# A two-layer hybrid block in fp32: the rests of block-product chunks behind the next down weights, and a block-product chunk in the first net

## The chip, the cores and the metric

The kernel runs on one core of one Trainium2 chip. A time is the device time of one execution in microseconds (us), and less is better. Several executions are given by their median. A profiled execution has a time of its own and a trace; the span is the stretch that the trace covers.

## The reference

All is fp32. One sequence of 256 tokens with 1024 features runs through two layers. This is the reference, cut to what matters here:

```python
def swiglu(x, w_gate, w_up, w_down):
    return (jax.nn.silu(x @ w_gate) * (x @ w_up)) @ w_down

for l in range(DEPTH):                       # DEPTH = 2, D_MODEL = 1024, D_FF = 2816
    h = layer_norm(ALPHA * h + 0.5 * swiglu(h, ffn1_gate[l], ffn1_up[l], ffn1_down[l]), ln_g[l, 0], ln_b[l, 0])
    z = h @ w_in[l]
    ...                                      # convolution, recurrence and pooling over parts of z
    h = layer_norm(ALPHA * h + mix, ln_g[l, 1], ln_b[l, 1])
    h = layer_norm(ALPHA * h + cross_attn(h, mem, ca_q[l], ca_k[l], ca_v[l], ca_o[l]), ln_g[l, 2], ln_b[l, 2])
    h = layer_norm(ALPHA * h + 0.5 * swiglu(h, ffn2_gate[l], ffn2_up[l], ffn2_down[l]), ln_g[l, 3], ln_b[l, 3])
```

`mem` has 256 rows of 1024. The change lies in `swiglu`, of which there are four; they are called nets here, and the first net is `ffn1` of layer 0.

## The kernel before

**Products.** An fp32 product is made of three TensorE (PE) products of parts. `split` makes the parts: ScalarE (ACT) casts the operand to a high part (L61), and VectorE (DVE) subtracts that from the operand for the low part (L62). Then high by high, high by low and low by high are added up in PSUM (`mm_rows`, all through L105). x is kept in such parts (`xTh`, `xTl`, both named xT in the profile). Weights come by DMA from SP's queue into a ring of six tiles `raw` (128x1024, 512 KB each), and their parts go into rings of eight `whi` and eight `wlo`. A DMA into `raw` must wait until both halves of the split have read the tile. PSUM has four `acc` and four `dn` tiles.

**A net.** D_FF is cut into five chunks of 512 columns and a last one of 256. A chunk c is made of x's products with gate and with up, then silu, then the product of the two; the outcome is turned so that its features lie across partitions: `turn` deals it out by four DMAs on SP (L450), DVE transposes it (L453), and it is split to `ah` and `al`. The down product then takes it in two halves, `both(c, 0)` and `both(c, 1)`. Each half is a slab of two weight tiles and 24 PE products, and all of them add to the four `dn` tiles. The program writes the half `both(c-2, 1)` and then `both(c-1, 0)` behind chunk c, so the down weights run about one chunk behind.

A chunk is made in one of two ways. `hidden` is the plain one: 48 PE products for gate and 48 for up. DVE multiplies at L440. `by_seven` takes gate and up together as a matrix of two by two blocks (`w00`, `w01`, `w10`, `w11`: gate and up, upper and lower half of x's features), x as two by two quarters, and makes their product by seven block products of 12 PE products each, 84 in all. For that DVE adds weight blocks to each other in place (L578), splits the sums as well (14 splits, where the plain chunk has 8), and combines the seven results (`put`, L600) into `e`, `f` and the two `g`; silu (L626) and a multiplication (L627) follow, then `turn`. `blocks_of_x` makes the four combinations of x's quarters that this needs (L536, L544 and a split each) and keeps them in `kTh` and `kTl`, which are otherwise used for the attention. Two of the quarters in fp32 are left over from the LayerNorm that made x (`pend(q[0:2])`).

```python
            sevens = (2, 4) if early is None else ()
```

So the third and fifth chunks of nets two to four are made by seven, and no chunk of the first net. `by_seven` loads its eight weight tiles into `spare0`, `spare1`, `spare2`, `lng`, `lnb` (tiles that LayerNorm's rows and other things use at other times) and three of `raw`.

**Beside it in the first net.** `early` is a function that only the first net gets. It issues the small parameters' and the memory's DMAs on GpSimd (POOL) behind the second chunk's weights (L193 for the memory, 32 of them), with the memory going to `spare0` and `spare1` (named m) and the parameters to `spare2`, and returns the `rest`: DVE's small steps and the memory's turning (L202, and four splits to mT). The rest is written behind the third chunk. `ln_params` loads the net's LayerNorm rows into `lng` and `lnb`, in the first net at c = 1, in the others at c = 5.

**Order.** A scheduler sets each engine's order from the program's order, with the dependences and buffers; every engine then runs its own list in order and waits at each entry for what it needs. `tc.issue_after` holds a piece back behind a given instruction, and in a `tc.manual_schedule` the written order stands.

Of the kernel before, what the change touches and what calls it, by code (L numbers as in the profile page):

```python
# [8 lines left out]
F32 = mybir.dt.float32  # L9
F32R = mybir.dt.float32r  # L10
U8 = mybir.dt.uint8
AF = mybir.ActivationFunctionType
# [5 lines left out]
P = 128  # L18
# [28 lines left out]
def model(ctx: ExitStack, tc: tile.TileContext, t: dict, out: bass.AP):  # L47
# [352 lines left out]
    def ffn(l, name, n, pend=None, last=False, early=None):  # L400
        gate, up, down = (t[f"{name}_{x}"][l] for x in ("gate", "up", "down"))
        with tc.tile_pool(name="ffn", bufs=2, reuse_waits="tile") as fp:
# [24 lines left out]
            def ordered(v):  # L427
                return v.rearrange("p (a k j) -> p k a j", a=4, j=32)
# [30 lines left out]
            def first():  # L459

                s = activations()
                wg = load(gate, 0, NK, 0, CHUNK, fine=pend is None)
                wu = load(up, 0, NK, 0, CHUNK) if pend is not None else None

                if pend is None:
                    idle = kTh[:, 0:2, :].rearrange("p k c -> p (k c)")
                    nc.vector.memset(idle.bitcast(F32), 0.0)

                    def busy(n):

                        for _ in range(n):
                            nc.tensor.matmul(blank, idle[:, 0:P], idle, start=True, stop=True)

                    with tc.manual_schedule(engines={E.Activation, E.DVE, E.PE}):
                        blank = acc((P, 512), "dn")
                        og = [acc((P, CHUNK), "dn") for _ in range(NT)]

                        def group(k, *tiles):
                            for i in tiles:
                                products(og[i], wg, i, k)  # L480

                        busy(5)
# [12 lines left out]
                        group(1, 1)  # L495
                        for k in range(2, NK):
                            if k + 1 < NK:
                                split(*wg.todo[k + 1])
                            group(k, 0, 1)
                    wu = load(up, 0, NK, 0, CHUNK)  # L500
                    ou = all_products(wu)
                    for i in range(NT):
                        activate(s, i, og[i])
                        gated(s, i, ou[i])
                else:
                    for i in range(NT):
                        og = acc((P, CHUNK))
                        for k in range(NK):
                            products(og, wg, i, k)
                        activate(s, i, og)  # L510
                        ou = acc((P, CHUNK))
                        for k in range(NK):
                            if i == 0 and k == NK // 2:
                                pend(q[0:2] if sevens else None)
# [4 lines left out]
            def hidden(c0):  # L519
# [11 lines left out]

            def blocks_of_x():

                for n, i, j in ((2, 0, 0), (3, 0, 1)):
                    part = (slice(None), slice(4 * j, 4 * j + 4), tok(i))
                    nc.vector.tensor_tensor(q[n], xTh[part].bitcast(F32), xTl[part].bitcast(F32), op=ALU.add)  # L536
                parts = [
                    tuple(y[:, 2 * n : 2 * n + 2, :].rearrange("p k (h t) -> p (k h) t", t=P) for y in (kTh, kTl))
                    for n in range(4)
                ]  # L540
                for n, o, a, b, op in (
                    (0, 1, 0, 1, ALU.subtract), (2, 0, 2, 0, ALU.subtract), (1, 2, 1, 2, ALU.subtract), (3, 3, 3, 2, ALU.add)
                ):
                    nc.vector.tensor_tensor(q[o], q[a], q[b], op=op)  # L544
                    split(*parts[n], q[o])
                return parts

            def by_seven(c0, bx):
# [50 lines left out]
                def put(o, a, op, b):  # L599
                    nc.vector.tensor_tensor(halves(o), sums(a), halves(b), op=op)  # L600
# [22 lines left out]
                s = fp.tile([P, NT, CHUNK], F32, tag="spare2", name="sg", bufs=1)  # L623
                for i, u in enumerate((e, f)):
                    v = ordered(s[:, i, :])
                    nc.scalar.activation(v, g[i].rearrange("p (k a j) -> p k a j", a=4, j=32), AF.Silu)  # L626
                    nc.vector.tensor_tensor(v, v, u.rearrange("p (k a j) -> p k a j", a=4, j=32), op=ALU.mult)  # L627
                return turn(s)

            def last_hidden(c0):  # L630

# [24 lines left out]
            if sevens:  # L656

                d = [fp.tile([P, DM], F32, tag=f"spare{n}", name="quarters", bufs=1) for n in range(2)]
                q = [d[n // 2].rearrange("p (n k t) -> p n k t", n=2, t=P)[:, n % 2] for n in range(4)]

            chunks = [(c, min(CHUNK, DFF - c)) for c in range(0, DFF, CHUNK)]

# [6 lines left out]
            def both(c, u):  # L669
                a = slab(c, u)  # L670
                for i in range(NT):
                    for k in range(2):
                        for m in range(2):
                            apart = last and i == m == k == u == 1 and c == 3
                            rows_of(a, i, k, m, c == u == k == 0, apart)

            for c, (c0, ncol) in enumerate(chunks):
                if not c:
                    acts.append(first())
                    ys = [[acc((P, 512), "dn") for _ in range(2)] for _ in range(NT)]  # L680
# [4 lines left out]
                if sevens and c == 1 and early is None:  # L685
                    bx = blocks_of_x()
                if c == (max(sevens) + 1 if sevens else 1):
                    gb = ln_params(l, n)
                if c == 1 and early is not None:

                    with tc.issue_after(loads[-1].ins):
                        rest = early(fp)
                if c == 2 and early is not None:
                    with tc.issue_after(lows[-1].ins):
                        for f in rest:
                            f()
                    if sevens:
                        bx = blocks_of_x()
# [485 lines left out]
```

## Time and profile before

| what | us |
|---|---|
| median of 3 runs | 1079.32 |
| lowest, highest | 1079.08, 1080.74 |
| profiled execution | 1079.12 |
| its span | 1077.2 |

In the profiled execution the granted TensorE clock was 0.999 of full speed, the program had 16293 instructions, and the DMA engines moved 231.9 MB, a mean of 215 GB/s. Rows of the profile name the line of the code, the engine, the operation, the tile written and, behind the arrow, the tiles read. A row of single instructions has its start in us and its duration first, and in brackets the idle time just before it and what ended that. PEld are PE's weight loads. Where a row stands for several instructions, x and their number follow.

### The profile page before, as it was taken

The page shows a single profiled execution, that of the slowest core. Times are in us where ns is not written, and L with a number is a line of the kernel's source. Part 1 is how long each engine was busy: PE and PEld are TensorE (multiplying, and loading weights), DVE is VectorE, ACT ScalarE, POOL GpSimd, SP SyncE. Part 2 cuts the span into 40 slices and gives each one's busy share as a digit, 9 for nine tenths or more (in the row PEclk, how much of TensorE's full clock was granted, in tenths as well). Part 3 has the DMA queues.
Part 4 walks back from the last instruction along what each step waited for, and adds up shares of the span by engine and source line. Part 5 has one row for each costly group of instructions (what it writes and reads, how often), then busy time and mean ns, then how long its engine had stood idle before and what let it go on. Part 6 is the DMA issues. An engine that isn't in the chain of part 4 may idle for free.

```text
span 1077.2 us, 16293 instructions
## 1 busy us (share of the span) xinstructions
PE 1064.0 (99%) x5979; PEld 939.5 (87%) x5979; DVE 921.3 (86%) x1287; ACT 630.2 (59%) x907; POOL 63.3 (6%) x114
## 2 busy tenths in 40 slices
PE   9999999999999999999999999999999999999997
PEld 7888888989899888888888888888898998888886
DVE  5758566998998799999799989888989787998986
ACT  6546454757467565555575556566764665655561
POOL 9600001000000000000000000010000000000000
PEclk9999999999999999999999999999999999999999
DMA  9997774754575575847675774956546665759371
GB/s 363 289 283 221 218 215 141 250 195 157 177 270 172 180 250 197 272 174 213 248 259 191 246 261 151 303 177 231 174 141 212 242 229 177 254 158 333 115 234 40
DMA packets 130895, 231.90 MB, mean 215 GB/s; under 512 B 9408, under 2 KB 48608, under 8 KB 130816
## 3 DMA queue, kind: packets, MB, share of 16 engines
q1 hardware_dynamic: 129024, 228.49, 64.9%
q0 software_dynamic: 1216, 1.20, 0.4%
q10 hardware_dynamic: 576, 1.18, 0.3%
q8 instruction: 47, 0.77, 0.3%
q14 instruction: 32, 0.26, 0.1%
HBM read 216.15 MB, written 1.05 MB: 202 GB/s over the span
## 4 chain that ended last, share of the span: by engine, by line
PE 88%; DVE 9%; issue 2%; ACT 0%; DMA 0%; DVEq 0%; ACTq 0%
PE acc L105 56%; PE dn L105 29%; DVE wlo L62 4%; DVE raw L578 2%; PE acc L172 1%; DVE half L600 1%; DVE square L453 1%; PE dn L886 1%; DVE al L62 1%; DVE sg L600 1%; DMA h<-in_x_dram 0%; PE dn L945 0%; ACT whi L61 0%; DVE sg L440 0%; DVE sg L627 0%
## 5 line engine op out<-in xcount | busy, mean ns | idle before, releaser
L61 ACT CAST whi<-raw 128x1024 fp32r<-128x1024 f32 (+1 forms) x432 | 435.3, 1042 | 227.6 <-DVE raw L578 74.0
L62 DVE TENSOR_TENSOR wlo<-raw,whi 128x1024 fp32r<-128x1024 f32 (+1 forms) x432 | 510.1, 1211 | 68.0 <-ACT whi L61 63.0
L105 PE MATMUL acc<-whi,xT 128*128 128x512 f32 x1072 | 324.6, 380 | 0.0
L105 PEld LDWEIGHTS acc<-whi,xT 128*128 128x128 f32 x1072 | 202.6, 189 | 28.6
L105 PE MATMUL acc<-wlo,xT 128*128 128x512 f32 x536 | 203.1, 379 | 0.0
L105 PE MATMUL acc<-xT,whi 128*128 128x512 f32 x576 | 142.2, 382 | 0.2
L105 PE MATMUL dn<-wlo,ah 128*128 128x512 f32 x346 | 131.8, 381 | 3.2 <-DVE wlo L62 3.2
L105 PE MATMUL dn<-whi,al 128*128 128x512 f32 x346 | 131.1, 379 | 0.0
L105 PE MATMUL dn<-whi,ah 128*128 128x512 f32 x346 | 130.5, 380 | 0.0
L105 PEld LDWEIGHTS acc<-xT,whi 128*128 128x128 f32 x576 | 103.9, 190 | 12.6 <-ACT whi L61 0.8
L105 PEld LDWEIGHTS acc<-wlo,xT 128*128 128x128 f32 x536 | 101.3, 189 | 14.5
L105 PE MATMUL dn<-whi,xT 128*128 128x512 f32 x288 | 88.4, 381 | 0.0
L105 PEld LDWEIGHTS acc<-xT,wlo 128*128 128x128 f32 x576 | 75.5, 191 | 3.9
L105 PEld LDWEIGHTS dn<-wlo,ah 128*128 128x128 f32 x346 | 65.4, 189 | 14.7 <-DVE wlo L62 5.6
L105 PE MATMUL acc<-xT,wlo 128*128 128x256 f32 x576 | 75.9, 275 | 0.0
L105 PEld LDWEIGHTS dn<-whi,ah 128*128 128x128 f32 x346 | 65.4, 189 | 9.2
L105 PEld LDWEIGHTS dn<-whi,al 128*128 128x128 f32 x346 | 65.4, 189 | 9.1
L350 POOL TENSOR_TENSOR rs<-rs,nhalf 128x1 f32<-128x1 f32 x16 | 14.9, 929 | 841.7 <-DVE rs L346 604.6
L105 PEld LDWEIGHTS dn<-whi,xT 128*128 128x128 f32 x288 | 54.4, 189 | 7.8 <-ACT whi L61 0.3
L578 DVE TENSOR_TENSOR raw<-raw 128x1024 f32<-128x1024 f32 x48 | 56.7, 1218 | 0.1
L105 PE MATMUL dn<-wlo,xT 128*128 128x512 f32 x144 | 54.8, 380 | 0.3 <-DVE wlo L62 0.3
L332 DVE SCALAR_TENSOR_TENSOR h<-h,dn 128x512 f32<-128x512 f32 x31 | 21.2, 683 | 28.6 <-PE dn L105 28.6
(232 smaller groups left out, 1232.2 us busy)
## 6 DMA issues: line engine op xcount, KB each, us to landing
raw<-in_ffn_up_dram SPq DMA_DIRECT2D x88, 512.0 KB, 5.4
raw<-in_ffn_down_dram SPq DMA_DIRECT2D x88, 512.0 KB, 6.3
raw<-in_ffn_gate_dram SPq DMA_DIRECT2D x84, 512.0 KB, 5.2
raw<-in_w_in_dram SPq DMA_DIRECT2D x48, 512.0 KB, 4.5
dealt<-sg SPq DMA_DIRECT2D x80, 128.0 KB, 4.4
raw<-in_ca_k_dram SPq DMA_DIRECT2D x16, 512.0 KB, 4.4
raw<-in_w_out_dram SPq DMA_DIRECT2D x16, 512.0 KB, 4.4
raw<-in_ca_v_dram SPq DMA_DIRECT2D x16, 512.0 KB, 5.4
```

What stands on the lines that cost most here:

```text
L61: nc.scalar.copy(hi, src)
L62: lows.append(nc.vector.tensor_tensor(lo, src, hi.bitcast(F32), op=ALU.subtract))
L105: nc.tensor.matmul(o, w, x, start=start, stop=stop)
L172: nc.tensor.transpose(pt[:, k, :], src[:, (4 * j + k) * P : (4 * j + k + 1) * P], unit)
L332: nc.vector.scalar_tensor_tensor(v, v, ALPHA / scale, sums(y[i][n]), op0=ALU.mult, op1=ALU.add, accum_out=None if junk is None else st[:, ...
L350: nc.gpsimd.tensor_tensor(rs, rs, nhalf[:, 0:1], op=ALU.pow)
L453: nc.vector.transpose(d.rearrange("p k (b r) -> p b k r", b=4), x[:, :, i, :].rearrange("p b (k j) -> p b k j", k=4))
L578: nc.vector.tensor_tensor(r[i], r[i], plus[i], op=ALU.add)
L600: nc.vector.tensor_tensor(halves(o), sums(a), halves(b), op=op)
L886: nc.tensor.matmul(o[g, hh, :], kc[:, hh, g], x, start=True, stop=True)
```

## The change

**The rests.** `by_seven` no longer does its last steps itself. It returns them as a function `left`: the last three `put`, both silu, both multiplications and `turn`. The loop calls it between `both(c-2, 1)` and `both(c-1, 0)`.

**The first net.** Its fifth chunk is made by seven (`sevens = (4,)`). x's four quarters are made from xT by four additions, since this x comes from no LayerNorm, and lie in `lng` and `lnb`. `hidden` takes a function that it calls between gate and up: in the second chunk that makes the blocks of x, in the third it is the `rest` with the memory's turning. `ln_params` moves to c = 5 as in the other nets. `by_seven` loads into the same tiles in all nets.

```diff
 def hidden(c0, between=lambda: None):
     ...
     for i in range(NT):
         activate(s, i, o[i])
+    between()
     o = all_products(load(up, 0, NK, c0, CHUNK))
 ...
 def blocks_of_x():
-    for n, i, j in ((2, 0, 0), (3, 0, 1)):
+    for n, i, j in ((2, 0, 0), (3, 0, 1)) + (((0, 1, 0), (1, 1, 1)) if early is not None else ()):
 ...
-    w00 = block(gate, 0, pieces("spare0", "spare1") if early is None else pieces("raw", "raw"))
+    w00 = block(gate, 0, pieces("spare0", "spare1"))
     w01 = block(up, 0, pieces("lng", "lnb"))
     w11 = block(up, 1, pieces("raw", "raw"))
-    w10 = block(gate, 1, pieces("spare2", "raw") if early is None else pieces("spare0", "spare1"))
+    w10 = block(gate, 1, pieces("spare2", "raw"))
 ...
     run(o[0], bx[3], parts_of(w11))
-    put(e, o[0], ALU.add, e)
     run(o[1], part_of_x(0, 1), parts_of(w10))
-    put(g[0], o[1], ALU.add, g[0])
     run(o[2], part_of_x(1, 1), parts_of(w00, w10))
-    put(g[1], o[2], ALU.add, g[1])
-    ...
-    return turn(s)
+    def left():
+        put(e, o[0], ALU.add, e)
+        for i in range(NT):
+            put(g[i], o[1 + i], ALU.add, g[i])
+        s = fp.tile([P, NT, CHUNK], F32, tag="spare2", name="sg", bufs=1)
+        for i, u in enumerate((e, f)):
+            v = ordered(s[:, i, :])
+            nc.scalar.activation(v, g[i].rearrange("p (k a j) -> p k a j", a=4, j=32), AF.Silu)
+            nc.vector.tensor_tensor(v, v, u.rearrange("p (k a j) -> p k a j", a=4, j=32), op=ALU.mult)
+        return turn(s)
+    return left
 ...
-sevens = (2, 4) if early is None else ()
+sevens = (2, 4) if early is None else (4,)
+bx = []
+if early is None:
     d = [fp.tile([P, DM], F32, tag=f"spare{n}", name="quarters", bufs=1) for n in range(2)]
+else:
+    d = [wp.tile([P, DM], F32, tag=g, name="quarters") for g in ("lng", "lnb")]
 ...
+def aside():
+    with tc.issue_after(lows[-1].ins):
+        if bx:
+            for f in rest:
+                f()
+        else:
+            bx.extend(blocks_of_x())
 ...
     elif c in sevens:
-        acts.append(by_seven(c0, bx))
+        left = by_seven(c0, bx)
     else:
-        acts.append(hidden(c0) if ncol == CHUNK else last_hidden(c0))
+        if c in (1, 2) and early is not None:
+            acts.append(hidden(c0, aside))
+        else:
+            acts.append(hidden(c0) if ncol == CHUNK else last_hidden(c0))
 ...
-    if c == (max(sevens) + 1 if sevens else 1):
+    if c == max(sevens) + 1:
         gb = ln_params(l, n)
-    if c == 2 and early is not None:
-        with tc.issue_after(lows[-1].ins):
-            for f in rest:
-                f()
     if c > 0:
         if c > 1:
             both(c - 2, 1)
+        if c in sevens:
+            acts.append(left())
         if c < len(chunks) - 1:
             both(c - 1, 0)
```

In the changed kernel L600 keeps its number, silu and multiplication are L629 and L630, and the lines of `blocks_of_x` are L537 and L545.

The scheduler moves instructions with it. The first place is DVE at the end of the second net's third chunk. half is the tile of `e` and `f`, sg that of the two `g`, acc a block product's outcome; `wlo<-raw,whi` is a split of a weight tile. Before:

```order
L600 TENSOR_TENSOR half<-acc,half 128x512
L62 TENSOR_TENSOR wlo<-raw,whi 128x1024
L600 TENSOR_TENSOR half<-acc,half 128x512
L600 TENSOR_TENSOR sg<-acc,sg 128x512
L62 TENSOR_TENSOR wlo<-raw,whi 128x1024
L627 TENSOR_TENSOR sg<-sg,half 128x4x4x32
L600 TENSOR_TENSOR sg<-acc,sg 128x512
L62 TENSOR_TENSOR wlo<-raw,whi 128x1024
L627 TENSOR_TENSOR sg<-sg,half 128x4x4x32
```

And after the change:

```order
L600 TENSOR_TENSOR half<-acc,half 128x512
L62 TENSOR_TENSOR wlo<-raw,whi 128x1024 x3
L600 TENSOR_TENSOR half<-acc,half 128x512
L600 TENSOR_TENSOR sg<-acc,sg 128x512 x2
L62 TENSOR_TENSOR wlo<-raw,whi 128x1024
L630 TENSOR_TENSOR sg<-sg,half 128x4x4x32 x2
```

The first split of each list is the last one of the chunk's own weights, and the next two are the two tiles of the down slab of `both(0, 1)`. Before, two of the rest's steps (L600 to half and to sg) stand between the chunk's last split and the slab's first, and two more (L627 and L600) between the slab's two; now all come behind both, the two L630 even behind the first tile of the next slab.

The second place is ACT at the same point. `whi<-raw` is the cast that each split begins with. Before:

```order
L61 CAST ah<-square 128x4x128 x2
L61 CAST whi<-raw 128x1024 x5
L626 ACTIVATE sg<-sg 128x4x4x32
L61 CAST whi<-raw 128x1024 x2
L626 ACTIVATE sg<-sg 128x4x4x32
```

And after:

```order
L61 CAST ah<-square 128x4x128 x2
L61 CAST whi<-raw 128x1024 x8
L629 ACTIVATE sg<-sg 128x4x4x32 x2
L61 CAST whi<-raw 128x1024 x3
L61 CAST ah<-square 128x4x128 x2
```

Both silu stand behind eight casts, where the first stood behind five and the second behind seven.

The third place is DVE in the first net's second chunk. Before:

```order
L62 TENSOR_TENSOR wlo<-raw,whi 128x1024 x11
L440 TENSOR_TENSOR sg<-acc,sg 128x2x4x32 x4
L62 TENSOR_TENSOR wlo<-raw,whi 128x1024 x4
L453 STREAM_TRANSPOSE square<-dealt 128x4x4x32 x2
L62 TENSOR_TENSOR al<-square,ah 128x4x128 x2
```

And after, with the steps of `blocks_of_x` among the splits (quarters are the quarters of x in fp32, kTh and kTl the parts of a block combination):

```order
L62 TENSOR_TENSOR wlo<-raw,whi 128x1024 x8
L537 TENSOR_TENSOR quarters<-xT 128x512 x4
L62 TENSOR_TENSOR wlo<-raw,whi 128x1024
L545 TENSOR_TENSOR quarters<-quarters 128x512
L62 TENSOR_TENSOR wlo<-raw,whi 128x1024
L440 TENSOR_TENSOR sg<-acc,sg 128x2x4x32 x2
L62 TENSOR_TENSOR kTl<-quarters,kTh 128x512
L440 TENSOR_TENSOR sg<-acc,sg 128x2x4x32 x2
L545 TENSOR_TENSOR quarters<-quarters 128x512
L62 TENSOR_TENSOR wlo<-raw,whi 128x1024
L62 TENSOR_TENSOR kTl<-quarters,kTh 128x512
```

Twelve steps on x come in between the eighth split and the first chunk's transposes; the memory's turning (L202), which stood behind the third chunk's transposes, moves up by one chunk, to those of the second.

More of the change, by code (lines that the diff above doesn't have):

```diff
@@ L513, in first @@
                             if i == 0 and k == NK // 2:
-                                pend(q[0:2] if sevens else None)
+                                pend(q[0:2])
                             products(ou, wu, i, k)
@@ L517, in first, with hidden @@
                 return turn(s)
-            def hidden(c0):
+            def hidden(c0, between=lambda: None):
                 s = activations()
@@ L617, in by_seven @@
                 run(o[0], bx[3], parts_of(w11))
-                put(e, o[0], ALU.add, e)
                 run(o[1], part_of_x(0, 1), parts_of(w10))
-                put(g[0], o[1], ALU.add, g[0])
                 run(o[2], part_of_x(1, 1), parts_of(w00, w10))
-                put(g[1], o[2], ALU.add, g[1])
[L623 to L627, printed above, removed]
-                return turn(s)
+                def left():
[9 more added lines that the diff above has]
+                return left
             def last_hidden(c0):
@@ L652, in slab @@
                 return w, ah[:, 2 * u : 2 * u + 2, :], al[:, 2 * u : 2 * u + 2, :]
-            sevens = (2, 4) if early is None else ()
-            if sevens:
+            sevens = (2, 4) if early is None else (4,)
+            bx = []
+            if early is None:
                 d = [fp.tile([P, DM], F32, tag=f"spare{n}", name="quarters", bufs=1) for n in range(2)]
-                q = [d[n // 2].rearrange("p (n k t) -> p n k t", n=2, t=P)[:, n % 2] for n in range(4)]
+            else:
+                d = [wp.tile([P, DM], F32, tag=g, name="quarters") for g in ("lng", "lnb")]
+            q = [d[n // 2].rearrange("p (n k t) -> p n k t", n=2, t=P)[:, n % 2] for n in range(4)]
             chunks = [(c, min(CHUNK, DFF - c)) for c in range(0, DFF, CHUNK)]
@@ L681, in ffn @@
                 elif c in sevens:
-                    acts.append(by_seven(c0, bx))
+                    left = by_seven(c0, bx)
                 else:
-                    acts.append(hidden(c0) if ncol == CHUNK else last_hidden(c0))
-                if sevens and c == 1 and early is None:
-                    bx = blocks_of_x()
-                if c == (max(sevens) + 1 if sevens else 1):
+                    if c in (1, 2) and early is not None:
+                        acts.append(hidden(c0, aside))
+                    else:
+                        acts.append(hidden(c0) if ncol == CHUNK else last_hidden(c0))
+                if c == 1 and early is None:
+                    bx.extend(blocks_of_x())
+                if c == max(sevens) + 1:
                     gb = ln_params(l, n)
```

2 lines of the change are left out of this document (removed).

## The prediction

> **What bounds the kernel now.** I read the page's busy shares first, then the chain of work that ended last, then single instructions of TensorE (PE), VectorE (DVE) and ScalarE (ACT) around the one place where the chain leaves PE.
>
> ```profile
> PE 1064.0 (99%) x5979; PEld 939.5 (87%) x5979; DVE 921.3 (86%) x1287; ACT 630.2 (59%) x907; POOL 63.3 (6%) x114
> PE 88%; DVE 9%; issue 2%; ACT 0%; DMA 0%; DVEq 0%; ACTq 0%
> ```
>
> PE is busy 99% of the span and carries 88% of the chain. The chain in order of time (start, length, what) shows where the other 9% lies:
>
> ```profile
> 50.20 5.18 PE dn L105 x24
> ...
> 76.21 10.36 PE dn L105 x48
> ...
> 117.65 20.72 PE acc L105 x96
> ...
> 437.21 1.13 DVE wlo L62
> ...
> 439.55 1.14 DVE wlo L62
> 440.73 8.69 PE dn L105 x39
> ...
> 480.50 18.13 PE acc L105 x84
> 498.63 10.36 PE dn L105 x48
> ```
>
> The reader is to see two things. First, PE's pace: 96 products of 512 columns take 20.72 us, 48 take 10.36, 84 take 18.13, each time 0.216 us a product, with the next piece starting where the last ends. The row of one product says 0.38 us, because products overlap; what one more or one fewer costs is 0.216. Secondly, in the second net's third chunk (made by seven block products) the chain leaves PE for DVE until 440.73. These are PE's own instructions there, and the page's row for such products over the whole run:
>
> ```profile
> 437.29 0.38 PE L105 MATMUL dn<-whi,ah 128*128 128x512 f32 x1
> 438.40 0.48 PE L105 MATMUL dn<-wlo,ah 128*128 128x512 f32 x1 [0.72 <-DVE wlo L62]
> 438.72 0.38 PE L105 MATMUL dn<-whi,al 128*128 128x512 f32 x1
> ...
> 439.58 0.81 PE L105 MATMUL dn<-whi,ah 128*128 128x512 f32 x3
> 440.73 0.48 PE L105 MATMUL dn<-wlo,ah 128*128 128x512 f32 x1 [0.34 <-DVE wlo L62]
> 441.05 0.38 PE L105 MATMUL dn<-whi,al 128*128 128x512 f32 x1
> L105 PE MATMUL dn<-wlo,ah 128*128 128x512 f32 x346 | 131.8, 381 | 3.2 <-DVE wlo L62 3.2
> ```
>
> Start to start, against 0.216 each: 438.40 - 437.29 loses 0.89, the next 0.10, 440.73 - 439.58 with three products loses 0.50, the next 0.10: 1.60 us. The idle shown is 0.72 + 0.34 = 1.06, and the page's 3.2 us is three times that: the nets two, three and four each have this stall, 4.8 us together. I found nothing else of that kind in any net.
>
> **Part 1: the rests behind the down weights (nets two to four).** What kept PE waiting is DVE's queue. DVE and ACT just there:
>
> ```profile
> 434.78 1.23 DVE L62 TENSOR_TENSOR wlo<-raw,whi 128x1024 fp32r<-128x1024 f32 x1
> 435.92 0.69 DVE L600 TENSOR_TENSOR half<-acc,half 128x512 f32<-128x512 f32 x1
> 436.52 0.69 DVE L600 TENSOR_TENSOR sg<-acc,sg 128x512 f32<-128x512 f32 x1
> 437.12 1.22 DVE L62 TENSOR_TENSOR wlo<-raw,whi 128x1024 fp32r<-128x1024 f32 x1
> 438.26 0.69 DVE L627 TENSOR_TENSOR sg<-sg,half 128x512 f32<-128x512 f32 x1
> 438.86 0.69 DVE L600 TENSOR_TENSOR sg<-acc,sg 128x512 f32<-128x512 f32 x1
> 439.46 1.22 DVE L62 TENSOR_TENSOR wlo<-raw,whi 128x1024 fp32r<-128x1024 f32 x1
> 433.70 3.89 ACT L61 CAST whi<-raw 128x1024 fp32r<-128x1024 f32 x4 [5.42 <-DVE raw L578]
> 437.50 0.62 ACT L626 ACTIVATE sg<-sg 128x512 f32<-128x512 f32 x1
> ```
>
> The splits at 437.12 and 439.46 are the two tiles of the down slab for which PE waits; two L600, then L627 and L600 stand ahead of them. In the new order the three splits follow each other, then come three L600, the third slab tile's split, two L630, and the fourth's. With DVE's steps as above (a split every 1.14, an L600 every 0.60): first slab tile 435.92 to 437.15, second 437.06 to 438.28, L600 at 438.2, 438.8 and 439.4, third tile 440.0 to 441.2. PE without a stall wants them at 437.29 + 0.216 = 437.51, 437.29 + 7 x 0.216 = 438.80 and, 24 products on, at 437.29 + 25 x 0.216 = 442.69. Leads: 0.36, 0.52, 1.5 us. ACT's order puts both silu behind seven casts from 433.70 on, not four: at 3.89 for four they end at 440.4, the silu run 440.4 to 441.5, and L630 can run at 441.2 and 441.8. The fourth tile is then split by 443.6, wanted at 442.47 + 7 x 0.216 = 443.98: a lead of 0.4. I take the stall as gone, -1.60 a net, **-4.80 us** in all; the bounds are 0 (it only moves one tile on) and -4.80, and thin leads are why the range reaches up. Next in line after that is the next chunk's gate weights, whose loads come free with the earlier splits. In SP's queue the four transfers of the gated chunk (L450) wait for the second L630, some 1.2 us later than for L627, and hold three up loads behind them; those weights are wanted half a chunk (10.4 us) after the gate's first, so I cost that at nothing. In chunk five the rest moves in the same way; DVE loses no work there, and PE had no stall.
>
> **Part 2: the first net's fifth chunk by seven products.** 84 products instead of 96: 12 x 0.216 = **-2.59 us** on PE. The Trainium skill (Perfetto Trace Analysis, Identifying the Most-Contended Engine) holds TensorE's busy share a poor measure of its limit and judges by the weight loads' share; that is 87% here, so by that rule PE has 13% free, twelve products are worth nothing, and the sum would end 2.59 higher, at 1074.5. The trace agrees that 99% says little, but its unbroken 0.216 us pace says that PE is the limit in this chunk, and I go by that.
>
> What pays for it is DVE. By these rows:
>
> ```profile
> 19.10:50.20 31.10, 31.10 (x146) 27.24 (x145) 22.76 (x24) 20.62 (x27) 23.51 (x41) 1.00 1.08 321
> 50.20:86.60 36.40, 36.40 (x170) 31.84 (x170) 23.51 (x30) 17.15 (x22) 0.23 (x1) 1.00 0.95 279
> 86.60:117.65 31.05, 31.05 (x145) 27.19 (x144) 24.09 (x44) 19.28 (x26) 0.00 (x0) 1.00 0.75 221
> 117.65:148.73 31.08, 31.08 (x145) 27.22 (x145) 18.50 (x21) 14.77 (x19) 0.00 (x0) 1.00 0.72 215
> 480.50:508.99 28.49, 28.49 (x133) 24.95 (x133) 28.28 (x31) 18.34 (x21) 0.00 (x0) 1.00 0.63 188
> L578 DVE TENSOR_TENSOR raw<-raw 128x1024 f32<-128x1024 f32 x48 | 56.7, 1218 | 0.1
> L440 DVE TENSOR_TENSOR sg<-acc,sg 128x256 f32<-128x256 f32 x56 | 20.3, 416 | 0.0
> 43.53 1.30 DVE L453 STREAM_TRANSPOSE square<-dealt 128x512 f32<-128x512 f32 x2 [2.82 <-DMA dealt<-sg]
> 45.12 1.29 DVE L62 TENSOR_TENSOR al<-square,ah 128x512 fp32r<-128x512 f32 x2 [0.29 <-ACT ah L61]
> 59.13 1.23 DVE L62 TENSOR_TENSOR wlo<-raw,whi 128x1024 fp32r<-128x1024 f32 x1 [0.97 <-ACT whi L61]
> 66.28 1.28 DVE L62 TENSOR_TENSOR al<-square,ah 128x512 fp32r<-128x512 f32 x2
> ```
>
> (The first five are stretches: length, then busy time and instructions of PE, weight loads, DVE, ACT, POOL.) Fifth chunk, DVE: 6 more splits x 1.22, 8 sums x 1.22, 9 L600/L630 x 0.69, less 4 L440 x 0.42 = 21.6 us. Its stretch (117.65 to 148.73) then holds 18.50 + 21.6 = 40.1 us of DVE for 28.5 us of PE, 11.6 too much. The cover is DVE's lead: the split that ends at 60.36 is the first of the slab that PE starts at 76.21, 15.8 us ahead, as far as eight buffers reach. The stretch before loses the memory's turning, 24.09 - 18.50 = 5.6 us, so the lead should be full. The second net's fifth chunk is the same work, 28.28 of 28.49 us busy, and the chain there shows PE straight on. Cost 0; with no lead at all, 11.6.
>
> x's blocks, now in chunk two (twelve 128x512 at 0.69 = 8.3 us): DVE has 31.10 - 22.76 = 8.3 free in that stretch, mostly ahead of 43.53, where it waited 2.82 for the first dealt chunk, and what it then makes (done at 46.4) is wanted from 50.20 on. Cost 0; with that cover gone, 8.3 less 3.8, or 4.5. The memory's 5.6 us fall into a stretch with 36.40 - 23.51 = 12.9 free: 0. ACT gains six casts, four of blocks and a copy, under 10 us, where it has over 10 free in each stretch: 0. Two 512 KB loads of LayerNorm rows leave the start for the fifth chunk, and the fifth chunk's weights go to tiles that the blocks and the memory have left; SP meets the gate's two of them between up loads of chunk four, and can wait there for the turning, some 3 us under a lead of 15: 0.
>
> **Sum.** The profiled execution took 1079.12 us with a span of 1077.2, so 1.9 lies outside. 1077.2 - 4.80 - 2.59 = 1069.8, plus 1.9 is 1071.7; the median shown is 0.2 above that execution: 1071.9.
>
> **Rivals.**
> (a) The stall moves on: the fourth slab tile's split stands behind two L630 that stand behind two silu and seven casts. For it: leads of 0.4 us. Against it: each step is a row's. The price is what it gives back, up to 1.60 a net: 1071.9 to 1076.7, at half 1074.3.
> (b) The first net gives its 2.59 back, because DVE's lead is short in its fifth chunk or the blocks are late in its second: 1074.5. For it, DVE 11.6 us over; against it the lead of 15.8.
> (c) Both, or the scheduled order runs otherwise than it reads and nothing comes of it: 1079.3.
> (d) Slower: DVE's queue, in order, reaches the memory's turning (behind the splits that end at 67.56) before the memory is there, and stands.
>
> ```profile
> L193 POOL DMA_DIRECT2D m<-in_mem_dram x32: 582/582/634, 24.6 to 49.8; - x32
> DMA to landing us min/median/max: 5.3/6.4/7.3
> ```
>
> Now it lands by 49.8 + 0.6 + 7.3 = 57.7, 9.9 us early. DVE's new work lies alongside POOL's issues. If each of the 32 waited for one split, 32 x 1.22 = 39 us, PE would lose 39 - 9.9 - 15.8 = 13.3: 1085.2. It decides from a delay of about 35 us on. The Trainium skill (SBUF — State Buffer, Who interferes with whom) has such a lock, DVE with two inputs in SBUF against a GpSimd instruction that reads it, the loser waiting in full. The rows speak against it: with DVE busy 22.76 us, the longest issue took 52 ns more than the median.
>
> **Chances.** Both parts as summed, to within 1.1 us: 0.70, with a range of its own of 1071.0 to 1073.0. (a) 0.12, (b) 0.10, (c) 0.05, (d) 0.03. Leaving out (c), (d) and the dearer half of (a), the range is 1071.0 to 1075.2. A measurement of this kernel tells about 0.2%, 2.2 us, from no change: faster 0.70 + 0.12 + 0.10 = 0.92, same 0.05, slower 0.03.
>
> **What would show it.** Part 1: in the chain DVE's pieces between the third and fourth chunk of nets two to four are gone, and the page's group dn<-wlo,ah has next to no idle; if the idle stands there but shorter, (a). Part 2: the first net's fifth chunk is a piece of 18.13 us with 84 products, the piece after it starting at its end; a gap there, or ahead of the first slab at 50.2, is (b). L202 near 67 without an idle ahead of it rules out (d). The forecast is wrong if PE waits somewhere that I cost at nothing.

## The result and the profile after

The changed kernel took 1072.25 us, the median of 6 runs (1071.58 to 1076.02), against 1079.26 before (6 runs); the ratio is 0.9938 with a 95% interval of 0.9923 to 0.9953. Forecast was 1071.9. Measured once more it took 1073.16 (5 runs, 1072.11 to 1074.17) against 1079.25, a ratio of 0.9942 [0.9930, 0.9955]. The profiled execution of the first measurement took 1073.05 with a span of 1071.0, 6.2 below the span of before, where 7.4 were forecast; so this execution lost 1.2 us somewhere that the sum had at nothing.

The page of the changed kernel: engines, the chain's shares, and the two groups of PE products that answer to the question (busy, mean ns | idle before, and what ended it).

```profile
PE 1060.4 (99%) x5967; PEld 938.2 (88%) x5967; DVE 945.5 (88%) x1318; ACT 642.4 (60%) x916; POOL 65.8 (6%) x114
PE 93%; DMA 3%; DVE 2%; ACT 1%; issue 1%; SPq 0%; DVEq 0%; ACTq 0%
L105 PE MATMUL acc<-whi,xT 128*128 128x512 f32 x1032 | 313.2, 380 | 1.1 <-ACT sg L436 1.1
L105 PE MATMUL dn<-wlo,ah 128*128 128x512 f32 x346 | 131.1, 379 | 0.0
```

The idle of 3.2 us in dn<-wlo,ah is gone. A new one of 1.1 us stands at acc<-whi,xT, ended by a silu (L436). The chain in order of time (start, length, what) puts that one in the first net and shows the second net unbroken:

```profile
67.53 0.56 ACT sg L436 x2
68.14 9.33 PE acc L105 x42
...
118.91 18.13 PE acc L105 x84
137.04 10.36 PE dn L105 x48
...
417.99 18.13 PE acc L105 x84
436.12 10.36 PE dn L105 x48
```

84 products in 18.13 us at 118.91 are the first net's fifth chunk, the next piece starting at its end: part 2 as forecast. At 417.99 the second net's third chunk now runs straight into its down slab: part 1 as forecast. DVE at that place, and the two PE products that want the slab's tiles:

```profile
433.45 3.49 DVE L62 TENSOR_TENSOR wlo<-raw,whi 128x1024 fp32r<-128x1024 f32 x3
436.86 0.68 DVE L600 TENSOR_TENSOR half<-acc,half 128x512 f32<-128x512 f32 x1
437.46 1.27 DVE L600 TENSOR_TENSOR sg<-acc,sg 128x512 f32<-128x512 f32 x2
438.66 1.21 DVE L62 TENSOR_TENSOR wlo<-raw,whi 128x1024 fp32r<-128x1024 f32 x1
439.79 1.28 DVE L630 TENSOR_TENSOR sg<-sg,half 128x512 f32<-128x512 f32 x2
436.17 0.38 PE L105 MATMUL dn<-wlo,ah 128*128 128x512 f32 x1
437.46 0.38 PE L105 MATMUL dn<-wlo,ah 128*128 128x512 f32 x1
```

The three splits from 433.45 end at 434.67, 435.81 and 436.94 (each a single row of the trace). The last two are the slab's tiles: 0.36 and 0.52 us ahead of PE at 436.17 and 437.46. The third and fourth tile came 1.48 and 0.44 ahead. The prediction had 0.36, 0.52, 1.5 and 0.4.

Now the new wait. The rows of the first net's third chunk: the small transposition on PE (L267) that belongs to the small parameters, PE's products around the wait, DVE's transposes of the dealt chunk, and ACT.

```profile
65.42 0.27 PE L267 MATMUL acc<-idn,rows 128*128 128x128 f32 x1
66.61 0.38 PE L105 MATMUL acc<-whi,xT 128*128 128x512 f32 x1
68.14 0.48 PE L105 MATMUL acc<-whi,xT 128*128 128x512 f32 x1 [1.14 <-ACT sg L436]
64.62 1.31 DVE L453 STREAM_TRANSPOSE square<-dealt 128x512 f32<-128x512 f32 x2 [4.42 <-DMA dealt<-sg]
65.37 1.21 ACT L61 CAST ah<-square 128x512 fp32r<-128x512 f32 x2 [3.88 <-DVE square L453]
67.44 0.65 ACT L436 ACTIVATE sg<-acc 128x256 f32<-128x256 f32 x2
```

PSUM has four `acc` tiles. A token tile is one half of the 256 tokens. Gate's two token tiles take two of the four, the transposition takes the third, up's first token tile the fourth; up's second token tile must have gate's first, and that is free when its silu (L436) has read it: the two silu from 67.44 end at 68.09, and PE goes on at 68.14. In ACT's list this silu stands behind the two casts to ah, which wait for the dealt chunk to land. Start to start 68.14 - 66.61 is 1.53 instead of 0.22, and the next product loses 0.10: 1.41 us. The rest of the way to the span's difference: -4.80 - 2.59 + 1.41 = -6.0, and 0.2 less at the very start of the program.

### The profile page after: what moved, and what is told of

The parts are those of the page before. It is cut to its first block, busy times and chain, and to the rows that moved or that the text cites. A ratio compares the mean times of both kernels' runs of the same rounds, so it can differ in the third digit from the quotient of the medians.

```text
span 1071.0 us, 16310 instructions
## 1 busy us (share of the span) xinstructions
PE 1060.4 (99%) x5967; PEld 938.2 (88%) x5967; DVE 945.5 (88%) x1318; ACT 642.4 (60%) x916; POOL 65.8 (6%) x114
## 3 DMA queue, kind: packets, MB, share of 16 engines
HBM read 216.15 MB, written 1.05 MB: 203 GB/s over the span
## 4 chain that ended last, share of the span: by engine, by line
PE 93%; DMA 3%; DVE 2%; ACT 1%; issue 1%; SPq 0%; DVEq 0%; ACTq 0%
PE acc L105 61%; PE dn L105 29%; PE acc L172 1%; DMA dealt<-sg 1%; DVE wlo L62 1%; DMA raw<-in_ffn_up_dram 1%; PE dn L902 1%; ACT whi L61 1%; DMA raw<-in_ffn_gate_dram 0%; PE dn L961 0%; DMA h<-in_x_dram 0%; DVE quarters L537 0%; ACT sg L436 0%; PE dn L950 0%; PE dn L960 0%
## 5 line engine op out<-in xcount | busy, mean ns | idle before, releaser
L61 ACT CAST whi<-raw 128x1024 fp32r<-128x1024 f32 (+1 forms) x438 | 442.7, 1041 | 203.6 <-PE dn L105 54.9
L105 PE MATMUL acc<-whi,xT 128*128 128x512 f32 x1032 | 313.2, 380 | 1.1 <-ACT sg L436 1.1
L105 PEld LDWEIGHTS acc<-whi,xT 128*128 128x128 f32 x1032 | 195.0, 189 | 29.1 <-ACT sg L436 1.5
L105 PE MATMUL acc<-wlo,xT 128*128 128x512 f32 x516 | 195.6, 379 | 0.0
L105 PEld LDWEIGHTS acc<-wlo,xT 128*128 128x128 f32 x516 | 97.5, 189 | 13.7
L578 DVE TENSOR_TENSOR raw<-raw 128x1024 f32<-128x1024 f32 x56 | 66.1, 1215 | 0.4
```

The lines of the kernel that those rows point to most:

```text
L61: nc.scalar.copy(hi, src)
L105: nc.tensor.matmul(o, w, x, start=start, stop=stop)
L578: nc.vector.tensor_tensor(r[i], r[i], plus[i], op=ALU.add)
```

## The experiments

Each kernel below is compared with the kernel before as measured beside it on the same chip: 1079.15 for the first four, 1079.25 for "both once more on one chip" and for the two with added steps, 1079.32 for the rest. Medians are of 4 to 11 runs.

**The first part alone.** The kernel before, with the rests as in the change; the first net plain.

```diff
+                def left():
+                    put(e, o[0], ALU.add, e)
+                    ...
+                    return turn(s)
...
                         both(c - 2, 1)
+                    if c in sevens:
+                        acts.append(left())
```

> The kernel before with the first part alone: the rests behind the down weights, the first net plain and the memory at its old place. If the stall of nets two to four is DVE's queue order and the order alone removes it: 3 x 1.60 us less, so about 1074.5 us, no idle in the group dn<-wlo,ah, and no wait of PE in the first net near 68 us. If the removed stall came back elsewhere (the rival a): 1075 to 1079, with idle of PE behind the third chunk of nets two to four.

Measured: 1074.17 (1074.10 to 1074.55), 4.98 below before; ratio 0.9955 [0.9942, 0.9967]. No idle is left in dn<-wlo,ah, and there is no wait near 68 us. Moving the rests is all that the stall needed. ACT's list changes with DVE's here; that it was DVE's that PE had waited for is read from the trace, and a doubled step on DVE, below, bears it out.

**The second part alone.** The changed kernel with the rests back in `by_seven`.

> The changed kernel with the rests put back in place: the first net's part alone. If the twelve products are worth their 0.216 us each: 2.59 us less than before, of which a wait of PE near 68 us (1.4 us in the profiled execution of the changed kernel) gives back from 0 to 1.4: 1076.7 to 1078.1, and the three stalls of 1.60 us are there as before. If PE's products are not what bounds the first net's fifth chunk: 1079.3 or more.

Measured: 1077.19 (11 runs, 1076.40 to 1081.11), 1.96 below before. Its profile has the chain's piece of 84 products in 18.13 us, the three old stalls, and the new wait, here 0.51 us of idle:

```profile
436.90 0.48 PE L105 MATMUL dn<-wlo,ah 128*128 128x512 f32 x1 [0.73 <-DVE wlo L62]
439.23 0.48 PE L105 MATMUL dn<-wlo,ah 128*128 128x512 f32 x1 [0.34 <-DVE wlo L62]
67.95 0.48 PE L105 MATMUL acc<-whi,xT 128*128 128x512 f32 x1 [0.51 <-ACT sg L436]
```

The two parts give 4.98 + 1.96 = 6.94. Both together gave 7.01, and 6.09 when measured once more (1079.25 - 1073.16), so they add up to within about 1 us.

**The small parameters behind the third chunk again.** The changed kernel with that one step put back; the memory's turning stays between gate and up.

```diff
                     if bx:
-                        for f in rest:
-                            f()
+                        rest[1]()
...
+                if c == 2 and early is not None:
+                    with tc.issue_after(lows[-1].ins):
+                        rest[0]()
```

> The changed kernel with one step put back: the small parameters (their PE transposition L267 and the small steps behind it) stand again behind the third chunk, the memory's turning stays between its gate and up. Theory (PSUM slot): the transposition takes the third of four acc tiles between gate and up, so up's second token tile has to take the gate's first tile and waits for its silu (L436); without it no PE wait near 68 us, 1071.6 us, and runs that differ less among each other. Rival (late transfer): ACT stands at the cast to ah until the dealt chunk lands at 64.5, and PE waits for that whoever has the slot: the wait of some 1.1 us stays, 1072 to 1073.

Measured: 1071.79 (1071.71 to 1073.11). PE goes on without a wait. This profile alone does not tell the slot from a late transfer: the dealt chunk came 1.33 us sooner than in the changed kernel's first profile (L453 at 63.29 against 64.62), and the two silu ended at 66.75, when PE would only just have wanted the tile. The same kernel's second profile (the variant under "both once more on one chip") does tell:

```profile
66.97 0.65 ACT L436 ACTIVATE sg<-acc 128x256 f32<-128x256 f32 x2
66.58 0.59 PE L105 MATMUL acc<-whi,xT 128*128 128x512 f32 x2
67.01 0.38 PE L105 MATMUL acc<-wlo,xT 128*128 128x512 f32 x1
```

Here the silu end at 67.62, and PE has gone on from 66.80 without a gap: its tile is the fourth one and does not hang on them.

**The same step moved in the kernel before.** Only the small parameters go between gate and up.

```diff
                     activate(s, i, o[i])
+                between()
...
+            def aside():
+                with tc.issue_after(lows[-1].ins):
+                    rest[0]()
...
                     with tc.issue_after(lows[-1].ins):
-                        for f in rest:
-                            f()
+                        rest[1]()
```

> The kernel before with only that step moved the other way: the small parameters between gate and up of the first net's third chunk, the memory's turning where it was. Theory (PSUM slot): PE now waits near 67 us for L436. In the profile of before the first two L436 end at 67.35 and PE reaches up's second token tile at about 67.05, so 0.3 us of idle and 0.1 for the restart if ACT's order stays; up to 1.4 as in the changed kernel: 1079.7 to 1080.7. Rival (late transfer alone, or the load of the fifth chunk's weights that the changed kernel issues at 50.06): no wait, 1079.3.

Measured: 1080.13 (11 runs, 1079.04 to 1081.71), 0.98 above before; ratio 1.001 [1.0001, 1.0018]. The wait appears in a kernel that has nothing else of the change, first its rows, then those of the kernel before:

```profile
66.79 1.19 ACT L436 ACTIVATE sg<-acc 128x256 f32<-128x256 f32 x4
67.49 0.48 PE L105 MATMUL acc<-whi,xT 128*128 128x512 f32 x1 [0.46 <-ACT sg L436]
```

```profile
66.75 1.20 ACT L436 ACTIVATE sg<-acc 128x256 f32<-128x256 f32 x4
66.66 0.59 PE L105 MATMUL acc<-whi,xT 128*128 128x512 f32 x2
```

The silu start at the same time in both, to 0.04 us. Without the slot PE starts its next product at 66.88; with it PE waits for the silu, and loses 0.73 us with the restart. So it is the slot, shown from both sides; the transfer only sets how long the wait is.

**Both once more on one chip.** The changed kernel, then the variant with the small parameters behind the chunk.

> The changed kernel once more, beside the next one on the same chip. The wait of PE near 68 us hangs on when the dealt chunk lands, so the runs should lie between 1071.5 (no wait) and 1073.1 (1.4 us, as in its profiled execution), median about 1072.2.

> The variant with the small parameters behind the third chunk, once more, beside the changed kernel on the same chip. If the PSUM slot was worth what it seems: lower than the changed kernel by 0.3 to 0.8 in the median and no run above it on that account; 1071.7. If the two don't differ: both 1072.0.

Measured: 1073.16 (1072.11 to 1074.17) and 1072.12 (1071.73 to 1074.17). The changed kernel's second profile has the wait at 0.19 us:

```profile
63.82 1.30 DVE L453 STREAM_TRANSPOSE square<-dealt 128x512 f32<-128x512 f32 x2 [3.47 <-DMA dealt<-sg]
67.33 0.48 PE L105 MATMUL acc<-whi,xT 128*128 128x512 f32 x1 [0.19 <-ACT sg L436]
```

The dealt chunk came 0.80 us sooner than in the first profile (63.82 against 64.62), and PE's wait is 0.95 shorter: the wait follows the landing. Start to start, and with the 0.10 of the next product, it cost 0.46 us. The variant's median is lower both times, by about 0.5 and 1.0, but the intervals overlap (0.9935 [0.9923, 0.9948] and 0.9936 [0.9924, 0.9949] against 0.9938 and 0.9942); by the times alone it would be unclear. And it has runs up to 1074.17 too, so the slot isn't the only thing that spreads them.

**The fifth chunk plain, blocks and memory moved.** The variant above, but no chunk of the first net is made by seven; x's block combinations are still made, and not used.

```diff
-                elif c in sevens:
+                elif c in sevens and (early is None or c != 4):
```

> The variant with the small parameters behind the third chunk, and the first net's fifth chunk plain again; x's block combinations are still made in the second chunk and not used, the memory is turned in the third. If the twelve steps on x and the earlier turning are hidden as the prediction costs them (0): the first part alone, 1074.2. And if the runs of the changed kernel differ by up to 2 us because the lead in the fifth chunk falls to 2 us, they lie as close as those of the first part alone (1074.1 to 1074.6). If the second and third chunk are the cause: median above 1074.4, and as wide as before.

Measured: 1074.40 (1074.09 to 1075.46), 0.2 above the first part alone, within the spread of either. The twelve steps on x and the earlier turning cost nothing that shows, and the fifth chunk by seven is worth 1074.40 less 1071.79 or 1072.12, so 2.3 to 2.6 us. Four of the five runs lie within 0.33 us and one is 1.04 above the next; the cause of the wide runs stays open.

**One step more ahead of the thin leads.** The first part alone, with the making of f doubled in the third chunk.

```diff
                 put(f, o[2], ALU.subtract, g[1])
+                if c0 == 2 * CHUNK:
+                    put(f, o[2], ALU.subtract, g[1])
```

> The first part alone, with one step of DVE doubled in the third chunk of nets two to four (the L600 that makes f runs twice, 0.60 us more of DVE just ahead of the chunk's last split and the down slab's splits; the outcome is the same). The leads in the trace of the changed kernel there: 0.20 us for the chunk's last split, then 0.36, 0.52, 1.48, 0.44 for the slab tiles. If these leads are all the cover there is, PE loses 0.60 - 0.20 = 0.40 a net and about 0.1 more for the restart: 3 x 0.5 = 1.5 above the first part alone at 1074.2, so 1075.4 to 1075.7. If PE is not waiting for DVE's list there: 1074.2. If every us of DVE counts in full: 1076.0.

Measured: 1076.16 (1075.80 to 1076.82), 1.99 above the first part alone, where 1.2 to 1.5 was expected. In the profile:

```profile
433.54 1.41 DVE L600 TENSOR_TENSOR half<-acc,sg 128x512 f32<-128x512 f32 x2
436.73 0.48 PE L105 MATMUL acc<-wlo,xT 128*128 128x512 f32 x1 [0.33 <-DVE wlo L62]
```

DVE's next step starts 1.32 us after the first of the two, where a single one takes 0.60, so the second cost 0.72; less the lead of 0.20 that is 0.52. PE lost 0.49 + 0.10 at this place, 1.8 for three nets. One single short step more on DVE, and 1.8 of the 4.8 us are given back: the leads are all the cover there is. The time alone would not tell this from the last case of the expectation, in which every us of DVE counts (three times 0.72 is 2.2); PE's rows do, since it lost 0.59 and not 0.72.

**Four steps more in the first net's fifth chunk.** On the variant with the small parameters behind the chunk.

```diff
                             nc.vector.tensor_tensor(r[i], r[i], plus[i], op=ALU.add)
+                            if i == 0 and plus is w10 and early is not None:
+                                for _ in range(4):
+                                    nc.vector.tensor_tensor(r[i], r[i], r[i], op=ALU.max)
```

> The variant with the small parameters behind the third chunk (1071.8), and four more DVE steps of 128x1024 (1.14 us each, the outcome the same) ahead of the last weight sum's split in the first net's fifth chunk. In the new order they and five L600 stand ahead of the split that PE takes next (start 128.69 in the profile without them, then 4 x 1.14 + 5 x 0.60 = 7.56 later, so ready at 137.5, wanted at 133.2). If the lead that the trace shows there (3.3 us in this chunk, down from 15) is all the cover: PE loses 4.3 us, 1076.1 to 1076.4. If the fifth chunk has cover beyond it: 1071.8 to 1073. If all of DVE's extra work counts: 4 x 1.14 on the path, no more than 1076.4 either, but with the wait spread over several tiles.

Measured: 1079.96 (11 runs, 1077.78 to 1080.69), 7.8 above the variant without them on the same chip (1072.12), where 4.3 to 4.6 was expected. PE around it, then stretches of time (length, then busy time and instructions of PE, weight loads, DVE, ACT and POOL, the granted clock, the DMA share and GB/s):

```profile
133.07 0.38 PE L105 MATMUL acc<-whi,xT 128*128 128x512 f32 x1
138.61 0.80 PE L105 MATMUL acc<-whi,xT 128*128 128x512 f32 x1 [5.16 <-ACT whi L61]
139.87 0.80 PE L105 MATMUL acc<-wlo,xT 128*128 128x512 f32 x1 [0.46 <-DVE wlo L62]
140.46 1.06 PE L105 MATMUL acc<-whi,xT 128*128 128x512 f32 x2
141.31 0.63 PE L105 MATMUL acc<-wlo,xT 128*128 128x512 f32 x1
...
132.00:139.00 7.00, 1.84 (x8) 1.23 (x6) 6.41 (x9) 1.49 (x2) 0.00 (x0) 0.85 0.23 80
139.00:144.20 5.20, 4.74 (x12) 3.54 (x12) 4.22 (x4) 5.20 (x7) 0.00 (x0) 0.55 0.14 30
144.20:150.00 5.80, 5.80 (x28) 5.09 (x27) 5.59 (x7) 4.12 (x5) 0.00 (x0) 1.00 0.82 242
```

The wait is 5.3 us, 1.0 more than worked out: the cast on ACT (1.05) between the sum and the split had been left out. What the expectation lacked altogether is the clock. From 139 to 144.2 it is granted at 0.55, and products start 0.43 us apart (140.46 to 141.31 holds two). Lost against 0.216 a product, from 130.6 to 143.8, are 8.4 us in all: 5.3 of the first wait, 1.0 of the second, the rest a slow PE.

**Third and fifth chunk of the first net by seven.** The memory is loaded behind the third chunk, into tiles that this chunk has left, and turned in the fourth; the small parameters come behind the fourth.

```diff
-            sevens = (2, 4) if early is None else (4,)
+            sevens = (2, 4)
...
-                    if c in (1, 2) and early is not None:
+                    if c in (1, 3) and early is not None:
...
+                if c == 2 and early is not None:
+                    with tc.issue_after(loads[-1].ins):
+                        rest = early(fp)
```

> The first net's third chunk by seven as well as its fifth, the memory loaded behind the third chunk and turned in the fourth. Twelve more products fewer: 2.59 less, 1069.2, if DVE's lead covers it. By the sum of DVE's work it doesn't: a lead of 10 to 15 us at the third chunk less 11.6, then 31.1 - 18.5 - 5.6 = 7 back in the fourth chunk, then 11.6 and 1 to 2 of small steps again: 2 to 5 us short in the fifth, which PE waits and then runs slowly for, as in the run with four more steps (5.3 us of waiting cost 8). 1071 to 1076.

Measured: 1105.01 (4 runs), 25.7 above before and far above what was expected. DVE's list reaches the memory's turning before the memory is there. The rows are DVE's stand, one of PE's two long waits that follow, and the chain that led to it:

```profile
123.82 0.71 DVE L202 STREAM_TRANSPOSE turned<-m 128x512 f32<-128x512 f32 x1 [14.46 <-DMA m<-in_mem_dram]
143.16 0.80 PE L105 MATMUL acc<-whi,xT 128*128 128x512 f32 x1 [7.34 <-ACT whi L61]
130.75 4.06 DMA m<-in_mem_dram
137.69 0.71 DVE turned L202
138.42 3.54 DMA raw<-in_ffn_gate_dram
```

DVE stands 14.46 us at the place that the prediction's rival (d) names, in a kernel that does start the memory late: 32 loads, issued from 114.0 to 132.0. PE's wait comes by a second way, though. The fifth chunk's gate weights go to `spare0` and `spare1`, where the memory lies, so their load starts only when the last turning is done (138.40), and the cast for which PE waits needs that load. It is the wait on SP that the prediction named and costed at nothing, and in the changed kernel it does cost nothing. The waits in the third chunk, 8 us of idle in all, stand beside it.

**The last weight sum of each chunk on GpSimd.** On the variant with the small parameters behind the chunk.

```diff
-                            nc.vector.tensor_tensor(r[i], r[i], plus[i], op=ALU.add)
+                            (nc.gpsimd if plus is w10 else nc.vector).tensor_tensor(r[i], r[i], plus[i], op=ALU.add)
```

> The variant with the small parameters behind the third chunk, the last weight sum of each chunk by seven (two tiles of 128x1024) made by GpSimd. DVE is relieved of 2.28 us just ahead of the thin leads. No row here has the price on GpSimd: 128x1 takes 0.93 us, a memset of 128x1024 0.95. Up to some 4 us for both tiles PE still gets them in time: 1071.7 or a little less, runs closer together. At 8 us or more for both, the last split of each of seven chunks comes late by 2 to 6 us: 1085 to 1110.

Measured: 1077.91 (11 runs, 1076.89 to 1079.99), some 6 us slower than with the sum on DVE. GpSimd's sums, and DVE's rows beside the second one in the second net:

```profile
L578 POOL TENSOR_TENSOR raw<-raw 128x1024 f32<-128x1024 f32 x14 | 43.2, 3098 | 349.8 <-DVE wlo L62 346.2
419.43 3.29 POOL L578 TENSOR_TENSOR raw<-raw 128x1024 f32<-128x1024 f32 x1 [3.59 <-DVE wlo L62]
418.13 7.95 DVE L62 TENSOR_TENSOR wlo<-raw,whi 128x1024 fp32r<-128x1024 f32 x5
```

The same five splits in the variant without GpSimd:

```profile
417.05 5.76 DVE L62 TENSOR_TENSOR wlo<-raw,whi 128x1024 fp32r<-128x1024 f32 x5
```

They took 7.95 us beside GpSimd's sum and 5.76 without it. The whole difference lies in one of the five:

```profile
420.40 3.40 DVE L62 TENSOR_TENSOR wlo<-raw,whi 128x1024 fp32r<-128x1024 f32 x1
```

The other four took 1.21 to 1.23 us each. GpSimd's sum ran from 419.43 to 422.72, and this split ended 1.08 behind it, about the time that it takes alone. The sum itself took 3.29 us, where the shortest of the 14 took 2.36, and began 1 us before the split ahead of this one had ended. So the two do not run side by side: each seems to have waited for the other in turn. DVE was relieved of 2.28 us a chunk and lost 2.2 to this, and PE waits again in the third chunk of nets two to four, 1.5 us in each; the rest of the 6 us was not followed up.

## Why the prediction was right, and what it had wrong

**Part 1** (-4.80): right in mechanism and size; alone it measured -4.98. The four leads came out within 0.04 us of those worked out from the rows of DVE and ACT. Rival (a) did not come about, but the doubled step shows how near it was: from 0.2 us more on DVE it begins. One lead had not been counted: the chunk's own last split comes 0.20 us ahead of PE, less than any of the four.

**Part 2** (-2.59): PE's term is right (18.13 for 84), and so is the cover. DVE was busy for all of the chunk's stretch:

```profile
118.91:147.40 28.49, 28.49 (x133) 24.95 (x133) 28.49 (x32) 20.07 (x22) 0.00 (x0) 1.00 0.69 195
134.55 1.21 DVE L62 TENSOR_TENSOR wlo<-raw,whi 128x1024 fp32r<-128x1024 f32 x1
138.39 0.38 PE L105 MATMUL dn<-wlo,ah 128*128 128x512 f32 x1
```

The lead went from 15.8 (the split that ends at 103.17 for PE at 118.96) to 2.6 (135.76 for 138.39): 13.2 used up where 11.6 was worked out. That is rival (b) missed by 2.6 us. The fifth chunk by seven measured 2.3 to 2.6 us against the plain one, so PE's pace was the limit, as the trace had it. On the weight loads' share alone as the measure (the Trainium skill, Perfetto Trace Analysis, Identifying the Most-Contended Engine) the twelve products would have been worth nothing; the page names that share beside a second measure, the share of peak arithmetic, which the prediction left out.

**What failed** is the step "The memory's 5.6 us fall into a stretch with 36.40 - 23.51 = 12.9 free: 0". For DVE that holds: the moved work with nothing else in the first net cost 0.2 at most in the medians. But it counted DVE's time alone. With the memory's turning the small parameters moved as well, and they are not DVE's small steps alone, as the text ahead of the prediction has it: they have one PE product, which takes a PSUM tile between gate and up. By the prediction's own sign, PE waiting somewhere that was costed at nothing, this step was wrong. Its price was 1.41 and 0.46 us in the two profiles. In the sum it would have made 1072.4 to 1073.3. That the first median came within 0.4 us of the forecast is in part luck: the wait differs from one profiled execution to the other, and the second measurement, 1073.16, lies outside the 1071.0 to 1073.0 given for both parts as summed, though inside the whole range.

**Rival (d)** did not come about: the longest issue of the memory's loads took 634 ns as before, beside DVE's new work, and DVE reached L202 without idle:

```profile
L193 POOL DMA_DIRECT2D m<-in_mem_dram x32: 582/583/634, 27.1 to 49.9; - x32
68.16 1.30 DVE L202 STREAM_TRANSPOSE turned<-m 128x512 f32<-128x512 f32 x2
```

Both halves of that rival show up in other kernels here, though. DVE standing at L202 is shown by the kernel with two chunks by seven, where PE's long waits ended with the weights that were to follow the memory into its tiles. And DVE and GpSimd held each other up when GpSimd made sums: one split of 3.40 us beside a sum of 3.29. The lock (the Trainium skill, SBUF — State Buffer, Who interferes with whom), in which the loser waits in full, agrees with that split. It was a sum on GpSimd that met DVE there; the DMA issues on GpSimd took no longer than before.

The fastest kernel measured is the change with the small parameters put back behind the third chunk: 1071.79 and 1072.12.

## What to carry to other kernels

When a step is moved, list what it takes of every shared thing, not only of the engine that it loads: one small transposition in a ring of four PSUM tiles made PE wait for a silu that nobody had waited for. In an in-order list, work out the lead of each instruction that the bound engine waits for; here that gave four leads to within 0.04 us, and told both that the stall would go and how little was left. Work that goes in ahead of a lead of 0.2 us shows at once.

## What the runs showed of the hardware beyond that

- A wait of 1.3 us cost itself and 0.1 us. Around one of 5.3 us PE lost 8.4: the wait, a second one of 1.0, and some 2 us in which products started 0.43 us apart instead of 0.216, with a mean granted clock of 0.55 in the 5.2 us from 139.0 on. The Trainium skill (TensorE: Matmul & The Clock Gate, What's actually happening) has it that about 3.4 us of idling halve the clock and about as much work restores it; the two waits lie on either side of that bound as it says, and the slow stretch was somewhat longer.
- GpSimd took 3.1 us in the mean, 2.36 at the least, for a sum of two 128x1024 tiles in SBUF, DVE 1.22. One DVE split that began during such a sum took 3.40 us instead of 1.22; its neighbours took no longer than without it.
- The same DVE step done twice in a row, from the same PSUM tile into the same SBUF tile, cost 0.72 us for the second, where steps on different tiles follow each other every 0.60; which of the two tiles it is that counts was not tested.
